# A hybrid decoder step on one core: nine matmuls that nothing reads, another order of the first loads, and sums of squares on GpSimd

## The chip, the cores and the metric

The kernel runs on one core of a Trainium2 chip. A core has five engines that run side by side, each with its own list of instructions: TensorE (PE, matmuls; PEld is its weight load), VectorE (DVE), ScalarE (ACT), GpSimd (POOL) and SyncE (SP), which here issues almost all DMA transfers. They wait for each other by semaphores. The metric is the device time of one execution in microseconds (us).

## What is computed

One inference step of a one-layer decoder on 1056 tokens: 1024 prompt tokens, and 8 sequences of 4 sampled tokens. The part that matters here is the very beginning of the layer:

```
h    = x * rsqrt(mean(x*x) + eps) * norm1        # RMSNorm over 1024 channels
proj = h @ w_in                                  # 1024 -> z | x,B,C | dt | q | k | v
```

After it come a Mamba-2 head group (a short causal convolution, then a chunked scan), a sliding-window attention group, one output projection with the residual, a second RMSNorm, an up-projection with a short convolution and a gate, and a down-projection. Everything is in float32.

## The kernel before

**Precision and layout.** Activations stand with channels on the partitions: `x[k]` is a block of 128 channels by T = 1056 tokens, k = 0 to 7. Each operand of a large matmul is split into a high and a low part: ScalarE writes the high part with a Copy (`xh` of the activations, L182; `uh` of the weights, L116), VectorE writes what is left over (`xl`, L183; `ul`, L119), and `dense` (L147) issues three matmuls for each product: high by high, low by high, high by low.

**The opening (L207 to L245).** The normalization is not applied ahead of the projection. The projection starts on the raw rows times the norm's weight, and the factor 1/rms of each token is applied to its results. So two things are made in the same loop over the eight k:

- the split rows: `xr` is loaded (L222), ScalarE makes `xh` with the norm's weight from `colt` as its scale, VectorE makes `xl`. For k = 0 this goes in three pieces of PC = 352 tokens, for the others in one of 1056;
- the sum of squares: ScalarE squares `xr` into `sq` (L228; the first one straight into `ssum`, L225), and an addition puts it onto `ssum` (L229). `sq` has two buffers, so a third square has to wait until the first has been added.

Two units of weights (`w01`, 128 output channels each) are loaded in parts of 256 columns, one part of each for every second k, and split by `load_part` (L113 to L119).

The matmuls of these two units run k by k: for each k two units by three pieces of tokens by three products, 18 matmuls of 128x352, 144 in all. They write the PSUM tiles called `ps` and `two`. Behind them `stats` (L155) sums `ssum` over the channels with nine matmuls that have one column, VectorE makes `rstd` of it, and TensorE goes on with the key and value projection (`token_major`, L199), whose weights (`wkv`, three loads) use the same two `raw` buffers as `w01` did.

**What sets the order.** The program is written in the order of the source, and a scheduler then places the instructions of each engine by its own estimate of times, before the kernel is built. So a change at the start can move instructions much later in the program. Around the middle a list called `PLAN` sets in which order the scan, the convolution, the gates and parts of the output projection are put to the scheduler. In the up-projection (L989) `half_rstd` (sums at L851, broadcast at L858) belongs to the second RMSNorm of one half of the tokens.

**The very first instructions.** VectorE fills `ones` (L207). ScalarE does one Exp of a single column (L208), ahead of which its function table is loaded. SP issues the two weight parts of k = 0, then `colt`, then the three pieces of the first rows, then the rest (L115, L218, L222).

Of the kernel before, what the change touches and what calls it, by code (L numbers as in the profile page):

```python
# [9 lines left out]
F32 = mybir.dt.float32  # L10
F32R = mybir.dt.float32r
I32 = mybir.dt.int32
AF = mybir.ActivationFunctionType
ALU = mybir.AluOpType
# [4 lines left out]
T = 1056  # L19
NP = 1024  # L20
NS = 32
NB = 8
NPAIR = 22
EPS = 1e-6
NEG = -1e30
PC = 352
# [20 lines left out]
def kernel(ctx, tc, xT, wxbc, wkv, wq, wz, wout, wup, wdn, cols, rows, cst, idm,  # L47
# [3 lines left out]
    act, dve, pool, pe, sp = nc.scalar, nc.vector, nc.gpsimd, nc.tensor, nc.sync  # L51
# [6 lines left out]
    xpc, xp = opened("xp", bufs=8, side="right")  # L58
    yp = ctx.enter_context(tc.tile_pool(name="yp", bufs=8))
# [6 lines left out]
    pqc, pq = opened("pq", bufs=3, space=PSUM)  # L66
# [4 lines left out]
    def bank(p=None):  # L71
        if p is None:
            p = pm if pm2 is None or rot[0] % 8 < 3 else pm2
            rot[0] += 1
        return p.tile([128, 512], F32, tag="ps", name="ps")
# [4 lines left out]
    colt = const.tile([128, NCOL], F32, name="colt")  # L80
# [5 lines left out]
    ones = const.tile([128, 128], F32, name="ones")  # L86
    rstd_bc = mid.tile([128, T], F32, name="rstd_bc")
    rstd = const.tile([128, 9], F32, name="rstd")
# [20 lines left out]
    def unit():  # L109
        return (wr.tile([128, 1024], F32, tag="raw", name="raw"), wp.tile([128, 1024], F32R, tag="uh", name="uh"),  # L110
                wp.tile([128, 1024], F32R, tag="ul", name="ul"))

    def load_part(u, src, a, b, e=None):  # L113
        raw, hi, lo = (t[:, a:b] for t in u)
        sp.dma_start(out=raw, in_=src)  # L115
        act.activation(out=hi, in_=raw, func=AF.Copy)  # L116
        n = (b - a) // (1 if e else 1)
        for i in range(0, b - a, n):
            (e or dve).tensor_tensor(out=lo[:, i:i + n], in0=raw[:, i:i + n], in1=hi[:, i:i + n].bitcast(F32),  # L119
                                     op=ALU.subtract)  # L120
# [52 lines left out]
    def x_pair(p):  # L173
        return (p.tile([128, T], F32R, tag="xh", name="xh"), p.tile([128, T], F32R, tag="xl", name="xl"))
# [30 lines left out]


    dve.memset(ones, 1.0)  # L207
    act.activation(out=rstd[:, 0:1], in_=ones[:, 0:1], func=AF.Exp)  # L208
    x = [None] * 8
    with tc.tile_pool(name="st", bufs=1, side="right", reuse_waits="tile") as stp:  # L210
        ssum = stp.tile([128, T], F32, name="ssum")
        w01 = [unit(), unit()]
        for k in range(8):
            if k % 2 == 0:
                for m in range(2):
                    load_part(w01[m], wxbc[m][:, 128 * k:128 * k + 256], 128 * k, 128 * k + 256)
            if k == 0:
                sp.dma_start(out=colt, in_=cols)  # L218
            xr = yp.tile([128, T], F32, tag="y", name="xr")
            x[k] = x_pair(xp)  # L220
            for a, b in ([(0, PC), (PC, 2 * PC), (2 * PC, T)] if k == 0 else [(0, T)]):
                sp.dma_start(out=xr[:, a:b], in_=xT[k][:, a:b])  # L222
                split(xr[:, a:b], x[k], col(C_N1 + k), a, b)
            if k == 0:
                act.activation(out=ssum, in_=xr, func=AF.Square)  # L225
            else:
                sq = stp.tile([128, T], F32, tag="sq", name="sq", bufs=2)
                act.activation(out=sq, in_=xr, func=AF.Square)  # L228
                dve.tensor_tensor(out=ssum, in0=ssum, in1=sq, op=ALU.add)  # L229
        w01 = [u[1:] for u in w01]  # L230
        sp.dma_start(out=idt, in_=idm)
        wkvu = [load_unit(wkv[:, 3 * i:min(8, 3 * i + 3), :].rearrange("p k c -> p (k c)"), 264 * min(3, 8 - 3 * i))
                for i in range(3)]
        sp.dma_start(out=sstt, in_=sst)
        sp.dma_start(out=rowt, in_=rows)
        sp.dma_start(out=cs, in_=cst[:, 0:K_LOW])
        dve.tensor_scalar(out=chalf, in0=colt[:, C_CW:C_CW + 40], scalar1=0.5, scalar2=None, op0=ALU.mult)
        two = pc.tile([128, 2, 512], F32, tag="sc", name="two")
        ps01 = [[bank(pm) for _ in range(3)], [two[:, 0], two[:, 1], bank(pq)]]
        for k in range(8):  # L240
            for m in range(2):
                for p in range(3):
                    dense(ps01[m][p][:, :PC], wl(w01[m]), xr_(x, p), [k], first=k == 0, last=k == 7)
                if k == 7 and m == 0:
                    stats(stp, ssum, pq)  # L245
        kv0 = token_major(264, wkvu, 3, 0, bank(pq))
        bcast(pq)
# [52 lines left out]
    with tc.tile_pool(name="at", bufs=1, reuse_waits="tile") as at:  # L300
# [52 lines left out]
        with tc.tile_pool(name="kv", bufs=1, reuse_waits="tile") as kvp:  # L353
# [4 lines left out]
            for t in range(9):  # L358
                _, m = tw(t)
# [4 lines left out]
                                         in1=rowt[:m, R_DTB:R_DTB + 8], op0=ALU.mult, op1=ALU.add)  # L364
# [12 lines left out]
                              op=ALU.add)  # L377
# [6 lines left out]
                              op=ALU.mult)  # L384
            sp.dma_start(out=pk, in_=kall[:, 7, :])
            sp.dma_start(out=sk[:, 124:128, :], in_=kall[:NS, 8, :])
            for j in range(3):
                ps = bank(pq)
                ts_ = range(4 * j, min(9, 4 * j + 4))
                for i, t in enumerate(ts_):  # L390
                    _, m = tw(t)
                    pe.transpose(out=ps[:, i * 128:i * 128 + m], in_=kall[:m, t, :], identity=ident[:m, :m])
                a = 512 * j
# [23 lines left out]
            for j in (13, 11, 9, 7, 5, 3):  # L417
# [9 lines left out]
                              in1=b3(na.unsqueeze(1), 128, 9, 8), op=ALU.mult)  # L427
# [14 lines left out]
                      start=True, stop=True)  # L442
# [391 lines left out]
    ssum = [None, None]  # L834
# [424 lines left out]
```

## Time and profile before

| what | us |
|---|---|
| time, median of three runs | 1193.34 |
| lowest and highest of them | 1191.61, 1196.62 |
| the profiled execution, its own time | 1193.78 |
| span of the profiled execution, from its first to its last instruction | 1192.0 |
| busy in it: PE, DVE, ACT, POOL | 1150.6, 872.0, 504.7, 316.6 |

The profiled execution takes 1.8 us more than its span. A row of the timeline has the start in us from the span's start, the busy time in us, the engine, the line of the source, the operation, what it writes and reads, how many such instructions were merged (x), and in brackets the idle time of the engine just before and what ended it. A row of the windows has a stretch of time, its length, the busy time and the number of instructions of PE, PEld, DVE, ACT and POOL, the clock that TensorE was granted (1.00 is full), the busy share of the DMA engines and GB/s. Matmuls are pipelined, so the rate of TensorE is read from the distance between two starts and not from the duration of one.

### The profile page before, as it was taken

Reading aid. Unit: us, or ns where it says so; the run is one execution under the profiler, and the core shown is the slowest. Engines: PE = TensorE matmul, PEld = TensorE weight load, DVE = VectorE, ACT = ScalarE, POOL = GpSimd, SP = SyncE. Lnnn points to the kernel's source line nnn. Section 1 sums busy time; section 2 is a strip of 40 time slices with the busy share of each in tenths; the row PEclk is TensorE's granted clock in tenths of the full one; section 3 lists DMA queues with packets and bytes.
Section 4 is the critical chain, followed back from the end, with each engine's and each line's share of the span. In section 5 each row is a group of like instructions: output and inputs, shape, how many; then the busy total and the mean of one; then the engine's idle time right before and its main releaser. Section 6 shows DMA issues by size and latency. Waiting matters only on the chain.

```text
span 1192.0 us, 22098 instructions
## 1 busy us (share of the span) xinstructions
PE 1150.6 (97%) x8614; PEld 1108.3 (93%) x8614; DVE 872.0 (73%) x1755; ACT 504.7 (42%) x992; POOL 316.6 (27%) x455
## 2 busy tenths in 40 slices
PE   8999999989968999889999999999999999999998
PEld 8998888879957999789999999999999999999998
DVE  7678967566987578998776666666666787677764
ACT  7444544445462334555455554545454421112110
POOL 0123233143454000044343444434442111001000
PEclk9999999999999999999999999999999999999999
DMA  8111112122454523122222222222222944324203
GB/s 294 64 63 54 36 37 59 51 90 87 142 195 154 174 81 120 36 93 74 85 82 81 73 90 73 90 73 89 73 74 89 364 144 155 105 90 128 96 9 146
DMA packets 52361, 122.53 MB, mean 103 GB/s; under 512 B 9232, under 2 KB 19984, under 8 KB 52240
## 3 DMA queue, kind: packets, MB, share of 16 engines
q1 hardware_dynamic: 52256, 121.12, 29.6%
q8 instruction: 67, 1.10, 0.4%
q14 instruction: 38, 0.31, 0.1%
HBM read 94.86 MB, written 27.26 MB: 102 GB/s over the span
## 4 chain that ended last, share of the span: by engine, by line
PE 86%; DVE 9%; ACT 2%; issue 2%; DMA 1%; POOL 0%; SPq 0%; ACTq 0%; DVEq 0%
PE ps L147 39%; PE ps L989 32%; PE ps L199 6%; PE ps L525 1%; PE sc L503 1%; DVE au L935 1%; DVE x2l L883 1%; PE two L147 1%; DVE c L1031 1%; DMA raw<-in_wup 1%; PE ps L517 1%; PE yy L653 1%; PE st L660 0%; DMA gr<-gd 0%; PE px L611 0%
## 5 line engine op out<-in xcount | busy, mean ns | idle before, releaser
L989 PE MATMUL ps<-x2h,au 128*128 128x264 f32 x2464 | 456.6, 286 | 10.2 <-ACT au L934 3.1
L989 PEld LDWEIGHTS ps<-x2h,au 128*128 128x128 f32 x2464 | 383.8, 189 | 13.1 <-ACT au L934 4.0
L989 PE MATMUL ps<-x2l,au 128*128 128x264 f32 x1232 | 348.7, 285 | 0.2 <-DVE x2l L883 0.2
L989 PEld LDWEIGHTS ps<-x2l,au 128*128 128x128 f32 x1232 | 232.4, 189 | 0.6 <-DVE x2l L883 0.6
L1104 DVE TENSOR_TENSOR acc<-acc,ps 128x352 f32<-128x352 f32 x264 | 131.4, 518 | 66.4 <-PE ps L147 65.9
L147 PE MATMUL ps<-xh,uh 128*128 128x264 f32 (+3 forms) x528 | 164.1, 317 | 8.8 <-ACT xh L182 5.8
L147 PE MATMUL ps<-gh,ul 128*128 128x352 f32 x528 | 170.1, 322 | 0.0
L147 PE MATMUL ps<-gl,uh 128*128 128x352 f32 x528 | 170.0, 322 | 0.0
L147 PE MATMUL ps<-gh,uh 128*128 128x352 f32 x528 | 167.9, 322 | 1.1 <-ACT gh L179 1.1
L147 PE MATMUL ps<-xl,uh 128*128 128x264 f32 (+3 forms) x528 | 165.6, 314 | 0.0
L147 PE MATMUL ps<-xh,ul 128*128 128x264 f32 (+3 forms) x528 | 165.1, 313 | 0.0
L116 ACT ACTIVATE uh<-raw 128x1024 fp32r<-128x1024 f32 (+3 forms) x59 | 55.8, 953 | 193.6 <-PE ps L147 169.4
L1031 DVE SCALAR_TENSOR_TENSOR c<-u,colt,c 128x1072 f32<-128x1072 f32 x88 | 121.6, 1383 | 6.5 <-ACT c L1029 6.1
L147 PEld LDWEIGHTS ps<-xh,uh 128*128 128x128 f32 x528 | 101.3, 193 | 12.6 <-ACT xh L182 5.8
L935 DVE TENSOR_TENSOR au<-raw,au 128x512 fp32r<-128x512 f32 x115 | 80.0, 711 | 40.4 <-ACT au L934 40.2
L147 PEld LDWEIGHTS ps<-xl,uh 128*128 128x128 f32 x528 | 102.1, 193 | 1.8 <-POOL xl L180 0.4
L147 PEld LDWEIGHTS ps<-xh,ul 128*128 128x128 f32 x528 | 102.1, 193 | 1.5 <-issue 0.8
L147 PEld LDWEIGHTS ps<-gh,uh 128*128 128x128 f32 x528 | 98.8, 188 | 1.3 <-ACT gh L179 1.3
L147 PEld LDWEIGHTS ps<-gl,uh 128*128 128x128 f32 x528 | 99.2, 188 | 0.4
L147 PEld LDWEIGHTS ps<-gh,ul 128*128 128x128 f32 x528 | 99.3, 188 | 0.0
L934 ACT ACTIVATE au<-raw 128x512 fp32r<-128x512 f32 x115 | 71.1, 625 | 31.0 <-POOL raw L922 11.9
L119 DVE TENSOR_TENSOR ul<-raw,uh 128x1024 fp32r<-128x1024 f32 (+3 forms) x51 | 62.3, 1231 | 10.8 <-ACT uh L116 10.8
(295 smaller groups left out, 1884.2 us busy)
## 6 DMA issues: line engine op xcount, KB each, us to landing
raw<-in_wup SPq DMA_DIRECT2D x46, 512.0 KB, 3.6
gr<-gd SPq DMA_DIRECT2D x22, 528.0 KB, 5.3
gd<-c SPq DMA_DIRECT2D x22, 512.0 KB, 2.6
raw<-in_wdn SPq DMA_DIRECT2D x22, 512.0 KB, 3.6
raw<-in_wout SPq DMA_DIRECT2D x12, 512.0 KB, 3.5
acc<-in_xT SPq DMA_DIRECT2D x16, 264.0 KB, 5.4
accd<-acc SPq DMA_DIRECT2D x16, 264.0 KB, 2.6
acc<-accd SPq DMA_DIRECT2D x8, 528.0 KB, 8.8
```

The source lines that it names most:

```text
L116: act.activation(out=hi, in_=raw, func=AF.Copy)
L119: (e or dve).tensor_tensor(out=lo[:, i:i + n], in0=raw[:, i:i + n], in1=hi[:, i:i + n].bitcast(F32), op=ALU.subtract)
L147: pe.matmul(out=ps, lhsT=w(a, k), rhs=x(b, k), start=first and k == ks[0] and i == 0, stop=last and k == ks[-1] and i == 2)
L199: pe.matmul(out=ps[:m, :n], lhsT=x[k][c][:, a:a + m], rhs=w[k // nk][b][:, o:o + n], start=k == 0 and i == 0, stop=k == 7 and i == 2)
L503: pe.matmul(out=sb[:, v, c].rearrange("p i k -> p (i k)"), lhsT=qT[a][r, c], rhs=kT[b][r, o:o + 256], start=i == 0, stop=i == 2)
L517: pe.transpose(out=pt[:, h], in_=P[:, h], identity=ident)
L525: pe.matmul(out=po[64 * v:64 * v + 64, 0:256].rearrange("p (c q) -> p c q", c=2), lhsT=(vall[:, t - i] if i or not t else vdif[:, t - 1])[ ...
L934: act.activation(out=u[:, 0:512], in_=src, func=AF.Copy)
L935: dve.tensor_tensor(out=u[:, 512:1024], in0=src, in1=u[:, 0:512].bitcast(F32), op=ALU.subtract)
L989: pe.matmul(out=ps, lhsT=wgt[:, 512 * a + 128 * k:512 * a + 128 * k + 128], rhs=xx[b][:, k], start=opens and k == 0 and i == 0, stop=k == ...
L1031: dve.scalar_tensor_tensor(out=c[:, 0:n], in0=u[:, j:j + n], scalar=col(C_FW + 3 * m + j), in1=c[:, 0:n], op0=ALU.mult, op1=ALU.add)
L1104: dve.tensor_tensor(out=o, in0=o, in1=ps[:, :PC], op=ALU.add)
```

## The change

1. Ahead of everything TensorE gets nine matmuls of `ones` by `ones`, 128x128, into a PSUM tile that nobody reads.
2. The two weight parts of k = 0 are issued from ScalarE's queue, ahead of its table load. SP issues the first third of the first rows first, then `colt`, then the other two thirds.
3. In the source, the splits of the first weights now stand ahead of the splits of the first rows and behind the load of the first third; for the even k from 2 on the order of weights and rows stays.
4. The additions of squares of k = 1 to 5 go to GpSimd; those of k = 6 and 7 stay on VectorE.

```diff
+NWARM = 9
...
     def load_part(u, src, a, b, e=None):
         raw, hi, lo = (t[:, a:b] for t in u)
-        sp.dma_start(out=raw, in_=src)
+        if src is not None:
+            sp.dma_start(out=raw, in_=src)
         act.activation(out=hi, in_=raw, func=AF.Copy)
...
     dve.memset(ones, 1.0)
-    act.activation(out=rstd[:, 0:1], in_=ones[:, 0:1], func=AF.Exp)
     x = [None] * 8
+
+    idle = bank(pq)
+    for i in range(NWARM):
+        pe.matmul(out=idle[:, 0:128], lhsT=ones, rhs=ones, start=True, stop=True)
     with tc.tile_pool(name="st", bufs=1, side="right", reuse_waits="tile") as stp:
         ssum = stp.tile([128, T], F32, name="ssum")
         w01 = [unit(), unit()]
+        for m in range(2):
+            act.dma_start(out=w01[m][0][:, 0:256], in_=wxbc[m][:, 0:256])
+        act.activation(out=rstd[:, 0:1], in_=ones[:, 0:1], func=AF.Exp)
         for k in range(8):
-            if k % 2 == 0:
+            xr = yp.tile([128, T], F32, tag="y", name="xr")
+            x[k] = x_pair(xp)
+            if k == 0:
+                sp.dma_start(out=xr[:, 0:PC], in_=xT[k][:, 0:PC])
+                sp.dma_start(out=colt, in_=cols)
+                for m in range(2):
+                    load_part(w01[m], None, 0, 256)
+            elif k % 2 == 0:
                 for m in range(2):
                     load_part(w01[m], wxbc[m][:, 128 * k:128 * k + 256], 128 * k, 128 * k + 256)
-            if k == 0:
-                sp.dma_start(out=colt, in_=cols)
-            xr = yp.tile([128, T], F32, tag="y", name="xr")
-            x[k] = x_pair(xp)
             for a, b in ([(0, PC), (PC, 2 * PC), (2 * PC, T)] if k == 0 else [(0, T)]):
-                sp.dma_start(out=xr[:, a:b], in_=xT[k][:, a:b])
+                if k or a:
+                    sp.dma_start(out=xr[:, a:b], in_=xT[k][:, a:b])
                 split(xr[:, a:b], x[k], col(C_N1 + k), a, b)
...
-                dve.tensor_tensor(out=ssum, in0=ssum, in1=sq, op=ALU.add)
+                (pool if k < 6 else dve).tensor_tensor(out=ssum, in0=ssum, in1=sq, op=ALU.add)
```

The new lines push all later lines 12 further down in the source (L147 is L149 after the change, L222 is L234, L229 is L241, L851 is L863).

SP's queue at the start of the program, before (`raw` are the weight parts, `xr` the rows, pieces of 352 or a whole block of 1056):

```order
L115 DMA raw<-in_wxbc 128x256 x2
L218 DMA colt<-in_cols 128x241
L222 DMA xr<-in_xT 128x352 x3
L222 DMA xr<-in_xT 128x1056
L115 DMA raw<-in_wxbc 128x256 x2
L222 DMA xr<-in_xT 128x1056 x2
```

and now:

```order
L225 DMA xr<-in_xT 128x352
L226 DMA colt<-in_cols 128x241
L234 DMA xr<-in_xT 128x352 x2
L234 DMA xr<-in_xT 128x1056
L117 DMA raw<-in_wxbc 128x256 x2
L234 DMA xr<-in_xT 128x1056 x2
```

The first two weight parts have left the queue, so that every transfer behind them stands two places further ahead; the rest has kept its order.

VectorE at the start of the program, before (`ul` and `xl` are the low parts of weights and rows, `ssum<-ssum,sq` the additions of squares):

```order
L119 TENSOR_TENSOR ul<-raw,uh 128x256
L237 TENSOR_SCALAR chalf<-colt 128x40
L119 TENSOR_TENSOR ul<-raw,uh 128x256
L183 SCALAR_TENSOR_TENSOR xl<-xr,colt,xh 128x352 x3
L183 SCALAR_TENSOR_TENSOR xl<-xr,colt,xh 128x1056
L229 TENSOR_TENSOR ssum<-ssum,sq 128x1056
L119 TENSOR_TENSOR ul<-raw,uh 128x256 x2
L183 SCALAR_TENSOR_TENSOR xl<-xr,colt,xh 128x1056
L229 TENSOR_TENSOR ssum<-ssum,sq 128x1056
```

and now:

```order
L249 TENSOR_SCALAR chalf<-colt 128x40
L121 TENSOR_TENSOR ul<-raw,uh 128x256
L185 SCALAR_TENSOR_TENSOR xl<-xr,colt,xh 128x352
L121 TENSOR_TENSOR ul<-raw,uh 128x256
L185 SCALAR_TENSOR_TENSOR xl<-xr,colt,xh 128x352 x2
L185 SCALAR_TENSOR_TENSOR xl<-xr,colt,xh 128x1056
L121 TENSOR_TENSOR ul<-raw,uh 128x256 x2
L185 SCALAR_TENSOR_TENSOR xl<-xr,colt,xh 128x1056 x2
```

The first rows' low part has moved between the two weight parts, and the additions between the low parts are gone; GpSimd has five of them in a row, directly ahead of its first subtraction of weights.

TensorE much later, at the sums of the second RMSNorm for the second half of the tokens (`ps<-ones,ssum` are the sums, the others are matmuls of the up-projection), before:

```order
L851 MATMUL ps<-ones,ssum_5166 88x1 x5
L989 MATMUL ps<-x2h,au 128x264
L989 MATMUL ps<-x2l,au 128x264
L989 MATMUL ps<-x2h,au 128x264 x2
L989 MATMUL ps<-x2l,au 128x264
L989 MATMUL ps<-x2h,au 128x264 x2
L989 MATMUL ps<-x2l,au 128x264
L989 MATMUL ps<-x2h,au 128x264 x2
L989 MATMUL ps<-x2l,au 128x264
L989 MATMUL ps<-x2h,au 128x264
L851 MATMUL ps<-ones,ssum_5166 88x1
```

and now:

```order
L1001 MATMUL ps<-x2l,au 128x264
L1001 MATMUL ps<-x2h,au 128x264 x2
L1001 MATMUL ps<-x2l,au 128x264
L1001 MATMUL ps<-x2h,au 128x264
L863 MATMUL ps<-ones,ssum_5176 88x1 x6
L1001 MATMUL ps<-x2h,au 128x264
L1001 MATMUL ps<-x2l,au 128x264
```

The six sums now stand together, behind more of the up-projection. From the 145th matmul of the before kernel to the middle of the scan TensorE's order is unchanged; from there to the early up-projection it differs in many small places like this one, and behind them it is the same again.

## The prediction

> **What bounds the kernel now.** I read the page first, then TensorE's waits in the opening, then the opening by windows and by timeline.
>
> ```profile
> PE 1150.6 (97%) x8614; PEld 1108.3 (93%) x8614; DVE 872.0 (73%) x1755; ACT 504.7 (42%) x992; POOL 316.6 (27%) x455
> PE 86%; DVE 9%; ACT 2%; issue 2%; DMA 1%; POOL 0%; SPq 0%; ACTq 0%; DVEq 0%
> ...
> PE ps L147 <- ACT xh L182: 5.8, 1, 5.8
> ```
>
> TensorE is busy for 97% of the span and is 86% of the chain that ended last. Of the 41.4 us in which it is idle, the first 5.8 us are the wait for the first rows. This and the rate of the first matmuls are what the change can touch directly, and all that it can save in the opening lies within these rows:
>
> ```profile
> 0.00:5.80 5.80, 0.00 (x0) 0.00 (x0) 1.17 (x8) 2.96 (x6) 0.69 (x7) 1.00 0.63 172
> 5.80:10.90 5.10, 5.10 (x19) 5.10 (x19) 2.38 (x4) 3.93 (x5) 0.00 (x0) 1.00 0.93 325
> 10.90:31.20 20.30, 20.30 (x128) 20.16 (x127) 20.11 (x23) 16.22 (x22) 0.00 (x0) 1.00 0.79 302
> 31.20:33.13 1.93, 1.93 (x21) 1.90 (x19) 0.00 (x0) 0.10 (x1) 0.00 (x0) 1.00 0.82 194
> 33.13:39.53 6.40, 5.93 (x35) 5.44 (x33) 3.45 (x18) 2.81 (x6) 2.71 (x5) 0.73 0.42 147
> ```
>
> The columns after the length are PE, PEld, DVE, ACT, POOL, the clock, the DMA share and GB/s. From 5.80 TensorE never stops until the sums at 31.20. But VectorE is busy 20.11 of 20.30 us beside it: two engines are full here, not one. TensorE's starts show the rate:
>
> ```profile
> 5.80 0.66 PE L147 MATMUL ps<-xh,uh 128*128 128x352 f32 x1 [5.80 <-ACT xh L182]
> ...
> 8.90 0.49 PE L147 MATMUL ps<-xl,uh 128*128 128x352 f32 x1
> 9.20 0.49 PE L147 MATMUL ps<-xh,ul 128*128 128x352 f32 x1
> 10.90 0.64 PE L147 MATMUL ps<-xh,uh 128*128 128x352 f32 x3
> 11.71 0.32 PE L147 MATMUL ps<-xl,uh 128*128 128x352 f32 x1
> 13.79 0.64 PE L147 MATMUL ps<-xh,uh 128*128 128x352 f32 x3
> 16.81 0.64 PE L147 MATMUL ps<-xh,uh 128*128 128x352 f32 x3
> 19.68 0.64 PE L147 MATMUL ps<-xh,uh 128*128 128x352 f32 x3
> 31.20 1.99 PE L155 MATMUL ps<-ones,ssum 128*128 128x1 f32 x18
> ```
>
> At 8.90 two starts are 0.30 us apart. The 18 matmuls of k = 0 take 5.80 to 10.90, 5.10 us; those of k = 3 take 16.81 to 19.68, 2.87 us or 0.159 each. The first 4.6 us or so run at half rate, though the clock column reads 1.00 there. Behind the sums it happens again, and there the column does show it (0.73 over 6.40 us, which costs 0.27 x 6.40 = 1.7 us).
>
> Does the slow start cost its 5.10 - 2.87 = 2.23 us? That depends on when the rows of k = 1 are there:
>
> ```profile
> 2.11 1.85 SPq L222 DMA_DIRECT2D xr<-in_xT  x4
> ...
> 0.73 1.28 ACT L208 ACT_TABLE_LOAD   x1 [0.73 <-PEq L1234]
> 2.86 0.94 ACT L116 ACTIVATE uh<-raw 128x256 fp32r<-128x256 f32 x2 [0.63 <-DMA raw<-in_wxbc]
> 5.16 1.07 ACT L182 ACTIVATE xh<-xr,colt 128x352 fp32r<-128x352 f32 x2 [1.36 <-DMA xr<-in_xT]
> 7.22 0.59 ACT L182 ACTIVATE xh<-xr,colt 128x352 fp32r<-128x352 f32 x1 [1.00 <-DMA xr<-in_xT]
> 7.72 1.07 ACT L225 ACTIVATE ssum<-xr 128x1056 f32<-128x1056 f32 x1
> 8.96 1.18 ACT L182 ACTIVATE xh<-xr,colt 128x1056 fp32r<-128x1056 f32 x1 [0.17 <-DMA xr<-in_xT]
> 10.04 1.07 ACT L228 ACTIVATE sq<-xr 128x1056 f32<-128x1056 f32 x1
> ...
> 10.17 1.32 DVE L183 SCALAR_TENSOR_TENSOR xl<-xr,colt,xh 128x1056 fp32r<-128x1056 f32 x1 [1.74 <-ACT xh L182]
> ```
>
> ScalarE waits for the last third of k = 0 until 7.22 and for the rows of k = 1 until 8.96. Their high part is ready at 10.14, their low part at 10.17 + 1.32 = 11.49. TensorE takes up that low part at 11.71, five matmuls into k = 1: it arrives just in time. So the slow matmuls of k = 0 are almost wholly hidden behind the loading of rows. The point that bounds the opening is 11.49, a DMA followed by ScalarE and VectorE.
>
> **The change part by part.**
>
> *Nine idle matmuls.* In the row at 31.20 a float32 matmul leaves two records: 18 for nine, in 1.93 us, 0.107 each, with 128 columns of weights to load. The nine new ones are 18 records too. Their price is at least 18 x 0.107 = 1.9 us, and 3.9 us if at half rate everything takes twice as long. They need only `ones`, ready at 1.0 us, so they end between 2.9 and 4.9 us, while TensorE would wait for rows anyway: cost nothing. Without that cover they would cost these 1.9 to 3.9 us. If 4.6 us of work release the full rate, as at the first matmuls, k = 0 runs fast from about 5.6 on.
>
> *Loads.* SP issues one transfer in about 0.45 us (1.85 us for four). The rows of k = 1 were its seventh transfer, issued at 2.11 + 3 x 0.46 = 3.5; now they are its fifth, at 0.74 + 4 x 0.45 = 2.55, so 0.95 us earlier, and so is the last third of k = 0. On ScalarE two issues at SP's price push the table load from 0.73 to about 1.6 and the first weight split from 2.86 to about 3.1; it has waited for its rows until 5.16, so this is covered. The weights are no later, since they are still issued at 0.74. How much earlier do the rows land? No earlier if the DMA engines are the limit: the bytes ahead of them are the same, and in 5.80:10.90 their share is 0.93. At most 0.95 us if the issue is the limit. In the first window it is 0.63 over 5.8 us, including the start, so some time is free: I take 0.6 us. Then the last third comes at 6.6, ScalarE's squares follow, the high part of k = 1 is ready at 9.5, the low part at 10.9. TensorE starts with the first rows at about 5.2 (their bytes share the engines with the weights), has finished k = 0 at about 8.8, and then waits for ScalarE and VectorE. This is the new wait: a fast TensorE meets rows that come only 0.6 us earlier. Gain 0.6 us, and not 2.23.
>
> *Additions on GpSimd.* VectorE loses five of seven additions:
>
> ```profile
> L229 DVE TENSOR_TENSOR ssum<-ssum,sq 128x1056 f32<-128x1056 f32 x7 | 8.8, 1254 | 0.1
> L119 POOL TENSOR_TENSOR ul<-raw,uh 128x1024 fp32r<-128x1024 f32 x8 | 19.1, 2391 | 37.4 <-ACT uh L116 37.2
> L922 POOL TENSOR_TENSOR t<-t,raw 128x512 f32<-128x512 f32 x20 | 28.5, 1425 | 88.6 <-DVE au L935 88.6
> ```
>
> That is 5 x 1.25 = 6.3 us, from 20.11 to 13.8 of 20.30. The only stall that this can remove is at k = 2: 13.79 to 16.81 is 3.02 us against 2.87, so 0.15 us.
> On GpSimd one addition costs 1056/1024 x 2.391 = 2.47 us by the first row, 1056/512 x 1.425 = 2.94 us by the second, whose stage has a busy VectorE as here. I take 2.94. The first square is ready at 11.1 - 0.6 = 10.5, so the fifth addition ends at 10.5 + 5 x 2.94 = 25.2. ScalarE's last square waits for it (`sq` has two buffers; behind it are the first splits of `wkv`): 26.3. VectorE's two additions end at 26.3 + 1.25 = 27.6. TensorE wants the sum at 31.20 - 0.75 = 30.4: 2.8 us to spare. The splits of rows for k = 6 and 7 stand ahead of the squares that wait. So this is hidden, cost nothing.
>
> *What follows.*
>
> ```profile
> 28.26 1.84 ACT L116 ACTIVATE uh<-raw 128x792 fp32r<-128x792 f32 x2 [2.88 <-DMA raw<-in_wkv]
> 33.03 0.64 ACT L116 ACTIVATE uh<-raw 128x528 fp32r<-128x528 f32 x1 [2.93 <-DMA raw<-in_wkv]
> ```
>
> The next weights, `wkv`, waited for a DMA, which waits until VectorE frees the `raw` buffers. VectorE gets there earlier now, so they come at least as early as TensorE does.
>
> *Order further on.* The scheduler has moved many instructions in the scan and the early up-projection. TensorE is not always busy there:
>
> ```profile
> 320.00:340.00 20.00, 15.88 (x118) 13.25 (x118) 14.74 (x24) 13.18 (x34) 10.21 (x16) 0.91 0.78 251
> 340.00:360.00 20.00, 15.14 (x145) 12.31 (x143) 19.87 (x49) 11.16 (x31) 9.78 (x13) 1.00 0.34 118
> 480.00:500.00 20.00, 16.36 (x116) 15.33 (x115) 19.30 (x34) 10.82 (x22) 0.00 (x0) 0.91 0.15 54
> 500.00:520.00 20.00, 15.79 (x121) 14.73 (x119) 18.48 (x30) 12.88 (x20) 4.82 (x6) 1.00 0.15 54
> ```
>
> It is idle 4.1 + 4.9 + 3.6 + 4.2 = 16.8 us, beside a VectorE that is nearly full in three of the four. The same work in another order can win or lose a part of this; I allow a fifth, 3.4 us, to either side, and take zero.
>
> **Sum.** Against the profiled execution: 1193.78 - 0.6 - 0.15 = 1193.03. It stands 0.44 above the median of 1193.34, so the forecast is 1192.6 us. This is far inside 0.5% (6 us, about what a measurement of this kernel can tell from no change).
>
> **The rivals.**
>
> *Rows come no earlier (chance 0.15).* Ends at 1193.34 - 0.15 = 1193.2. For it: the share of 0.93 in 5.80:10.90. Against it: the idle DMA time ahead of 5.80. [...] No run here shows yet which of the two it is. The same end comes if the idle matmuls do not release the clock: k = 0 from 5.2 at 0.29 each ends at 10.4, and little of the 0.6 is left.
>
> *The slow start counts in full (0.12).* If rows came as early as TensorE wants them, it would save 2.23 us of slow matmuls and 5.80 - 4.8 = 1.0 us of waiting: 1193.34 - 3.2 = 1190.1. For that the low part of k = 1 would have to be ready at 8.3 and its rows at 5.8, where now they land at 8.96. Against it: two transfers fewer in SP's queue do not give 3 us.
>
> *The order further on decides (0.15).* 3.4 us to either side: 1189.2 or 1196.0.
>
> *GpSimd holds up the sums (0.08), slower than before.* From 10.5 + 5 d + 1.07 + 1.25 = 30.4 on, which is d = 3.5 us an addition, TensorE waits at the sums and everything behind waits with it. Each further 0.1 us of d costs 0.5 us; at d = 4.9 it is 6.9 us, 1192.6 + 6.9 = 1199.5. For it: GpSimd shares the stretch with a VectorE at work, and its 128x512 row is slower there. Against it: even that row gives 2.94.
>
> **How the numbers follow.** The forecast case has 0.50. The range goes from the full slow start with an order that helps, 1190.1 - 3.1 = 1187.0, to no gain with an order that hurts, 1193.3 + 3.4 = 1196.7. Faster by over 0.5% means under 1187.4, which only two favourable cases together reach: 0.10. Slower by over 0.5% means over 1199.3: GpSimd, or an order that does worse than I allow: 0.07. The rest, 0.83, is the same.
>
> **What would show it.** Right: 18 records of idle matmuls that end before 5; matmul starts 0.16 apart from about 5.6; a wait of TensorE for `xh` or `xl` of k = 1 near 9 to 11; the sums near 30.4; GpSimd's additions under 3.5 us each and VectorE near 14 us in that stretch. Wrong: a TensorE that goes through k = 1 without a wait at full rate (the second rival); starts still 0.29 apart at 8 us; a wait of the sums (L157) for VectorE's additions; or an opening that is shifted by 0.75 us and an end that is not, which puts the cause into the order further on.

## The result and the profile after

The changed kernel takes 1207.4 us (median of six, 1201.2 to 1211.8), the kernel before 1191.2 (six): a ratio of 1.0122, 95% interval 1.0093 to 1.0151 (the two medians alone divide to 1.0136). A second series gave 1207.8 and 1.0131 (1.0097 to 1.0165). Single executions of some kernels fell to a clock of 0.65 to 0.85; they count in the medians of the table below, but not in its ratios, its half-rate loss or its stages, and so one of its rows has no stages. The changed kernel is slower by 1.2%; the forecast was "the same", and its range ended at 1196.7. The profiled execution takes 1206.67 us, its span is 1204.9 against 1192.0.

The opening by windows, changed kernel, cut where TensorE starts the first rows, takes up the low part of k = 1, starts the sums and leaves them:

```profile
0.00:5.33 5.33, 4.21 (x18) 3.92 (x18) 0.74 (x7) 2.54 (x5) 0.70 (x7) 1.00 0.69 203
5.33:10.64 5.31, 4.61 (x24) 3.98 (x24) 3.27 (x6) 4.79 (x8) 0.35 (x1) 1.00 0.97 351
10.64:37.67 27.03, 21.58 (x122) 21.27 (x122) 24.78 (x17) 15.77 (x21) 13.88 (x5) 0.87 0.63 233
37.67:39.59 1.92, 1.92 (x20) 1.89 (x18) 0.00 (x0) 0.46 (x1) 0.00 (x0) 1.00 0.48 166
```

Up to the low part of k = 1 the change does what it says: 10.64 against 11.71 us before. The same matmuls then take 27.03 us; before, 31.20 - 11.71 = 19.49. TensorE is idle for 5.45 of them and its clock is 0.87. VectorE should have been relieved; it is busy 24.78 us with fewer instructions than before. TensorE's waits up to the sums name it:

```profile
PE ps L149 <- DVE xl L185: 5.7, 2, 5.4
...
PE ps L149 <- ACT xh L184: 0.4, 1, 0.4
```

And the timelines of VectorE and of GpSimd, changed kernel, tell why (start, busy, engine, line, operation, what it writes and reads, how many merged):

```profile
9.27 1.32 DVE L185 SCALAR_TENSOR_TENSOR xl<-xr,colt,xh 128x1056 fp32r<-128x1056 f32 x1 [2.04 <-ACT xh L184]
10.54 5.24 DVE L121 TENSOR_TENSOR ul<-raw,uh 128x256 fp32r<-128x256 f32 x2
15.71 6.90 DVE L185 SCALAR_TENSOR_TENSOR xl<-xr,colt,xh 128x1056 fp32r<-128x1056 f32 x2
22.53 3.01 DVE L121 TENSOR_TENSOR ul<-raw,uh 128x256 fp32r<-128x256 f32 x2
25.47 2.54 DVE L185 SCALAR_TENSOR_TENSOR xl<-xr,colt,xh 128x1056 fp32r<-128x1056 f32 x2
...
10.29 5.21 POOL L241 TENSOR_TENSOR ssum<-ssum,sq 128x1056 f32<-128x1056 f32 x2 [9.06 <-ACT sq L240]
15.65 9.28 POOL L241 TENSOR_TENSOR ssum<-ssum,sq 128x1056 f32<-128x1056 f32 x3 [0.15 <-ACT sq L240]
```

Read the two engines side by side. The two small `ul` subtractions last 10.54 to 15.78, GpSimd's first two additions 10.29 to 15.50. The two `xl` of 15.71 to 22.61 stand beside the next additions. GpSimd ends at 24.93, and from 25.47 on two `xl` take 2.54 us again, 1.27 each. A short VectorE instruction that meets an addition on GpSimd lasts here until that addition is over: the two `ul` take 2.66 and 2.65 us, where two of the same size took 0.42 us each ahead of the additions (4.72 and 5.81), and each ends 0.28 us after the addition that it met.

The kernel before shows the same thing at two places, neither of which the prediction read. VectorE and GpSimd, kernel before:

```profile
63.54 3.13 DVE L119 TENSOR_TENSOR ul<-raw,uh 128x1024 fp32r<-128x1024 f32 x1 [2.26 <-ACT uh L116]
...
63.18 2.40 POOL L119 TENSOR_TENSOR ul<-raw,uh 128x1024 fp32r<-128x1024 f32 x1
...
93.59 2.30 DVE L140 SCALAR_TENSOR_TENSOR qv<-rs 128x8 f32<-128x8 f32 x1
...
93.46 2.41 POOL L119 TENSOR_TENSOR ul<-raw,uh 128x1024 fp32r<-128x1024 f32 x1 [0.82 <-ACT uh L116]
```

An instruction with eight columns that takes 2.30 us, and ends 0.02 us after GpSimd does (95.89 and 95.87), is not at work: it is waiting inside its own busy time. (The same instruction takes 0.17 us at 80.09, with no GpSimd instruction beside it.)

Behind the opening the trace is later by another 6.4 us. Windows from the sums to the scan, to the end of it and of the output projection, to the end of the up-projection, and to the end; kernel before, then the changed one:

```profile
31.20:279.00 247.80, 239.46 (x1759) 214.10 (x1757) 176.51 (x537) 116.04 (x318) 70.08 (x107) 0.97 0.18 57
279.00:463.80 184.80, 172.53 (x1410) 159.91 (x1410) 142.46 (x343) 82.98 (x180) 47.80 (x73) 0.98 0.43 140
463.80:934.50 470.70, 459.22 (x3722) 455.72 (x3721) 341.32 (x521) 240.11 (x419) 180.51 (x252) 1.00 0.24 85
934.50:1192.00 257.50, 254.00 (x1588) 253.36 (x1586) 188.06 (x322) 42.48 (x44) 17.51 (x17) 1.00 0.37 131
```

```profile
37.67:284.80 247.13, 238.19 (x1759) 212.69 (x1757) 178.21 (x537) 115.39 (x318) 70.20 (x107) 0.98 0.18 56
284.80:474.70 189.90, 178.23 (x1410) 163.25 (x1410) 141.03 (x343) 81.67 (x179) 50.13 (x73) 0.96 0.41 136
474.70:947.40 472.70, 461.09 (x3722) 457.84 (x3721) 335.45 (x521) 242.05 (x420) 184.53 (x252) 0.99 0.26 85
947.40:1204.90 257.50, 253.97 (x1588) 253.33 (x1586) 188.65 (x322) 42.48 (x44) 17.90 (x17) 1.00 0.37 131
```

The opening costs 37.67 - 31.20 = 6.5 us, the scan 5.1, the up-projection 2.0; from the sums to the scan 0.7 comes back. In the scan TensorE is not idle for longer (11.7 us against 12.3); it is busy for longer, at a lower clock (0.96 against 0.98). This is where the scheduler has put TensorE's instructions in another order.

### The profile page after: what moved, and what is told of

It reads as the page before. It is cut to its first block, busy times and chain, and to the rows that moved or that the text cites. A ratio compares the mean times of both kernels' runs of the same rounds, so it can differ in the third digit from the quotient of the medians.

```text
span 1204.9 us, 22147 instructions
## 1 busy us (share of the span) xinstructions
PE 1161.9 (96%) x8632; PEld 1116.3 (93%) x8632; DVE 872.1 (72%) x1750; ACT 504.7 (42%) x992; POOL 337.7 (28%) x460
## 4 chain that ended last, share of the span: by engine, by line
PE 85%; DVE 8%; DMA 3%; ACT 2%; issue 1%; POOL 0%; SPq 0%; DVEq 0%; ACTq 0%; POOLq 0%
PE ps L149 38%; PE ps L1001 33%; PE ps L201 6%; DMA raw<-in_wup 1%; PE ps L537 1%; PE sc L515 1%; DVE au L947 1%; DVE x2l L895 1%; PE yy L665 1%; PE st L672 1%; PE ps L529 1%; PE two L149 1%; DMA h<-in_h0T 1%; PE yy L667 0%; DVE acc L882 0%
## 5 line engine op out<-in xcount | busy, mean ns | idle before, releaser
L149 PE MATMUL ps<-xl,uh 128*128 128x264 f32 (+3 forms) x528 | 166.6, 316 | 7.6 <-DVE xl L185 5.7
L149 PE MATMUL ps<-gh,ul 128*128 128x352 f32 x528 | 170.1, 322 | 0.0
L149 PE MATMUL ps<-gl,uh 128*128 128x352 f32 x528 | 170.0, 322 | 0.0
L149 PE MATMUL ps<-xh,uh 128*128 128x264 f32 (+3 forms) x528 | 163.8, 316 | 5.6 <-ACT uh L118 1.9
L149 PE MATMUL ps<-gh,uh 128*128 128x352 f32 x528 | 167.9, 322 | 0.6 <-ACT gh L181 0.6
L149 PE MATMUL ps<-xh,ul 128*128 128x264 f32 (+3 forms) x528 | 164.9, 313 | 0.0
L149 PEld LDWEIGHTS ps<-xl,uh 128*128 128x128 f32 x528 | 102.6, 194 | 11.2 <-DVE xl L185 6.3
L149 PEld LDWEIGHTS ps<-xh,uh 128*128 128x128 f32 x528 | 101.1, 193 | 10.6 <-issue 2.8
L149 PEld LDWEIGHTS ps<-xh,ul 128*128 128x128 f32 x528 | 102.4, 194 | 1.0 <-issue 0.2
L149 PEld LDWEIGHTS ps<-gh,uh 128*128 128x128 f32 x528 | 98.8, 188 | 0.9 <-ACT gh L181 0.9
L149 PEld LDWEIGHTS ps<-gl,uh 128*128 128x128 f32 x528 | 99.2, 188 | 0.4
L149 PEld LDWEIGHTS ps<-gh,ul 128*128 128x128 f32 x528 | 99.3, 188 | 0.0
L121 DVE TENSOR_TENSOR ul<-raw,uh 128x1024 fp32r<-128x1024 f32 (+3 forms) x51 | 65.2, 1287 | 10.1 <-ACT uh L118 10.1
```

The source lines that it names most:

```text
L149: pe.matmul(out=ps, lhsT=w(a, k), rhs=x(b, k), start=first and k == ks[0] and i == 0, stop=last and k == ks[-1] and i == 2)
```

## The experiments

**Theory A**: while an addition runs on GpSimd, VectorE's two-input instructions cannot run, so an addition costs VectorE's path GpSimd's 2.9 us in place of its own 1.25. **Theory B**: the new order of loads stretches VectorE. **Theory C**: the other order further on costs the rest, whatever the opening does. All runs of the decoder stand in one table; ratios are against the kernel before on the same chip. The three columns of stages are from one profile each, and a profiled execution can lie several us from its kernel's median (1206.6 against 1201.5 with the additions alone, 1188.5 against 1192.7 with the idle matmuls alone). The half-rate loss is the mean over the runs of (1 - granted clock) x span.

| kernel | median us | ratio (95%) | sums at | sums to scan | scan to end of up-proj. | half-rate loss |
|---|---|---|---|---|---|---|
| before | 1191 to 1193 | | 31.2 | 247.8 | 655.5 | 13 |
| changed | 1207.4 | 1.0122 (1.0093-1.0151) | 37.7 | 247.1 | 662.6 | 23.3 |
| changed, again | 1207.8 | 1.0131 (1.0097-1.0165) | 37.7 | 249.7 | 659.2 | 21.9 |
| before + additions on GpSimd | 1201.5 | 1.0074 (1.0049-1.0100) | 38.5 | 249.9 | 659.0 | 17.6 |
| two additions on GpSimd | 1203.6 | 1.0100 (1.0075-1.0125) | 34.1 | 250.0 | 660.3 | 18.6 |
| additions in quarters | 1200.7 | 1.0084 (1.0054-1.0115) | 34.5 | 247.0 | 658.5 | 18.0 |
| additions of one column | 1196.2 | 1.0034 (1.0015-1.0054) | 30.3 | 247.6 | 658.8 | 16.2 |
| one-input on GpSimd | 1197.5 | 1.0052 (1.0031-1.0073) | 30.1 | 246.7 | 661.7 | 17.3 |
| additions back on VectorE | 1188.5 | 0.9972 (0.9953-0.9990) | | | | 13.4 |
| the same, again | 1188.0 | 0.9965 (0.9949-0.9980) | 30.7 | 246.4 | 650.7 | 12.4 |
| loads only | 1191.1 | 0.9985 (0.9969-1.0002) | 30.8 | 244.7 | 653.8 | 13.9 |
| the same + k = 1 in thirds | 1190.2 | 0.9982 (0.9969-0.9994) | 30.3 | 247.7 | 655.0 | 13.4 |
| idle matmuls only | 1192.7 | 1.0000 (0.9977-1.0022) | 31.3 | 245.0 | 653.0 | 14.3 |

Behind the opening TensorE has one order of instructions in the changed kernel and in the kernels with additions in quarters, of one column and with one input, and another in the kernel before, with the idle matmuls alone and with k = 1 in thirds. The kernels with the additions alone, with two additions, and with the additions back on VectorE (with and without idle matmuls) have three further orders there.

### Additions back on VectorE, and the additions alone

```diff
-                (pool if k < 6 else dve).tensor_tensor(out=ssum, in0=ssum, in1=sq, op=ALU.add)
+                dve.tensor_tensor(out=ssum, in0=ssum, in1=sq, op=ALU.add)
```

> The changed kernel with all seven additions of squares back on VectorE; idle matmuls and new load order stay. Theory A (GpSimd's additions keep VectorE's two-input instructions out while they run: 0.38 us became 2.6, 1.3 became 3.45): VectorE's subtractions take 0.38 and 1.3 us again, TensorE's 5.4 us wait for the low part of k = 2 is gone, sums at 30 to 30.7 us instead of 37.67 (before: 31.20). Theory B (the new order of loads, not GpSimd, stretches VectorE: more transfers in flight beside it): VectorE stays stretched, sums near 37. Theory C (the scheduler's other order further on costs the other 6.4 us whatever the opening does): sums as in A, but the whole is still 4 to 7 us above the kernel before; by A alone it is 0 to 2 us below it, 1189 to 1191.

Repeated:

> The changed kernel with all additions on VectorE once more, for a profile at the usual clock. Theory A: VectorE's subtractions at 0.38 and 1.3 us, sums at 30.0 to 30.7; total 2 to 5 us below the kernel before as the first time.

The sums stand at 30.70, and VectorE, with the new loads beside it and 1.25 us more to do for each k, is quick again (timeline of the repeat):

```profile
10.89 1.25 DVE L241 TENSOR_TENSOR ssum<-ssum,sq 128x1056 f32<-128x1056 f32 x1
12.05 0.75 DVE L121 TENSOR_TENSOR ul<-raw,uh 128x256 fp32r<-128x256 f32 x2
12.73 1.31 DVE L185 SCALAR_TENSOR_TENSOR xl<-xr,colt,xh 128x1056 fp32r<-128x1056 f32 x1
```

The reverse edit puts only the additions of k = 1 to 5 of the kernel before on GpSimd:

```diff
-                dve.tensor_tensor(out=ssum, in0=ssum, in1=sq, op=ALU.add)
+                (pool if k < 6 else dve).tensor_tensor(out=ssum, in0=ssum, in1=sq, op=ALU.add)
```

> The kernel before with only the additions of k = 1 to 5 on GpSimd. Theory A: each addition keeps VectorE out for 2.9 us instead of using it for 1.25, 5 x 1.65 = 8.2 us on a VectorE that was busy 20.11 of 20.30 us: sums at 37.5 to 39.5 us, total 6 to 15 us slower than before. Theory B (loads): VectorE at 0.38 and 1.3 us, sums at 31.2, total the same within 2 us.

With the old loads VectorE is held as in the changed kernel, and the sums stand at 38.5 (timelines of VectorE and GpSimd):

```profile
11.52 5.22 DVE L119 TENSOR_TENSOR ul<-raw,uh 128x256 fp32r<-128x256 f32 x2
16.67 6.93 DVE L183 SCALAR_TENSOR_TENSOR xl<-xr,colt,xh 128x1056 fp32r<-128x1056 f32 x2
...
11.26 5.21 POOL L229 TENSOR_TENSOR ssum<-ssum,sq 128x1056 f32<-128x1056 f32 x2 [10.03 <-ACT sq L228]
16.64 9.31 POOL L229 TENSOR_TENSOR ssum<-ssum,sq 128x1056 f32<-128x1056 f32 x3 [0.17 <-ACT sq L228]
```

The additions alone make the loss of the opening, and the loads have no part in it. Theory B has fallen. What lies behind the sums cannot be compared so directly here, since this kernel has an order of its own there.

### Two additions, and additions in quarters

```diff
-                (pool if k < 6 else dve).tensor_tensor(out=ssum, in0=ssum, in1=sq, op=ALU.add)
+                (pool if k < 3 else dve).tensor_tensor(out=ssum, in0=ssum, in1=sq, op=ALU.add)
```

> The changed kernel with only the additions of k = 1 and 2 on GpSimd. Theory A, additive: 2 x 1.65 = 3.3 us on VectorE, sums at 33 to 34 us, between 30.3 (none) and 37.67 (five). Rival D (the loss is one event: the first long wait takes TensorE's clock, and the rest follows from that): sums near 37 already with two, or near 31 if two are not enough to make TensorE wait.

Sums at 34.13. From 30.70 with none, two additions cost 3.4 us, 1.7 each; the sum by A was 2 x 1.65 = 3.3. TensorE waits 3.3 us for the low part of k = 2 here and keeps its clock up to the sums, so the wait alone, without a loss of clock, shifts the opening: rival D has fallen. Its total (+11 us) is not explained by that; it has yet another order further on, and the longest way from the sums to the scan in the table (250.0).

```diff
-                (pool if k < 6 else dve).tensor_tensor(out=ssum, in0=ssum, in1=sq, op=ALU.add)
+                for c in range(0, T if k < 6 else 0, 264):
+                    pool.tensor_tensor(out=ssum[:, c:c + 264], in0=ssum[:, c:c + 264], in1=sq[:, c:c + 264], op=ALU.add)
+                if k > 5:
+                    dve.tensor_tensor(out=ssum, in0=ssum, in1=sq, op=ALU.add)
```

> The changed kernel with each addition on GpSimd cut into four pieces of 264 columns; the order of all other instructions is the changed kernel's. Theory A (exclusive use, one instruction at a time): no VectorE instruction is held longer than a quarter addition, 0.75 us and its own time, but GpSimd's total is the same or a little more, so the sums stay at 36.5 to 39 us. Rival E (VectorE is slowed only because it starves behind one long instruction, and shares well with short ones): sums at 31 to 33 us and most of the loss gone.

The sums come at 34.48, between the two expectations. GpSimd's and VectorE's timelines and TensorE's waits:

```profile
10.00 21.68 POOL L242 TENSOR_TENSOR ssum<-ssum,sq 128x264 f32<-128x264 f32 x20 [8.78 <-ACT sq L240]
...
12.01 3.54 DVE L185 SCALAR_TENSOR_TENSOR xl<-xr,colt,xh 128x1056 fp32r<-128x1056 f32 x2
15.47 1.88 DVE L121 TENSOR_TENSOR ul<-raw,uh 128x256 fp32r<-128x256 f32 x2
...
PE ps L157 <- DVE ssum L244: 2.8, 1, 2.8
PE ps L149 <- DVE xl L185: 1.4, 3, 0.7
```

Now the two engines take turns: `xl` takes 1.77 us instead of 3.45, and GpSimd is the one that is held, 21.68 us for what takes 14.5 in whole additions. TensorE waits only 1.4 us for low parts on its way through the rows, and stops for 2.8 us at the sums instead. Cutting the instructions moved the wait here, it did not remove it: both engines' work still lies end to end.

### What holds what

A kernel of its own, which computes nothing of the decoder, puts four VectorE instructions of one kind beside three GpSimd instructions of one kind.

> Nothing of the decoder is computed: four VectorE instructions of one kind stand beside three GpSimd instructions of one kind, 128x1056 float32, for six kinds of VectorE and four of GpSimd, and each kind alone. Theory A: subtraction and scaled subtraction on VectorE take 1.25 to 1.35 us alone and, beside GpSimd's addition, last as long as GpSimd's (2.5 to 3.5 us); beside GpSimd's one-input kinds and its fill they stay at 1.25 to 1.35. Multiplication with a PSUM input, one-input kinds and the fill on VectorE keep their time beside any of GpSimd's. Theory B (VectorE was stretched by transfers, not by GpSimd): no pair differs from VectorE alone by more than a tenth.

Its rows, VectorE first alone and then beside GpSimd's addition (128x1056; 128x512 where PSUM is read):

```profile
6.16 5.14 DVE L69 TENSOR_TENSOR vo<-va,vb 128x1056 f32<-128x1056 f32 x4
18.27 2.94 DVE L76 TENSOR_SCALAR vo<-va 128x1056 f32<-128x1056 f32 x4
25.76 2.87 DVE L82 TENSOR_TENSOR vo<-pt,va 128x512 f32<-128x512 f32 x4
...
43.37 11.40 DVE L69 TENSOR_TENSOR vo<-va,vb 128x1056 f32<-128x1056 f32 x4
67.82 9.20 DVE L76 TENSOR_SCALAR vo<-va 128x1056 f32<-128x1056 f32 x4
87.82 2.87 DVE L82 TENSOR_TENSOR vo<-pt,va 128x512 f32<-128x512 f32 x4
...
108.69 7.36 DVE L69 TENSOR_TENSOR vo<-va,vb 128x1056 f32<-128x1056 f32 x4
193.30 5.14 DVE L69 TENSOR_TENSOR vo<-va,vb 128x1056 f32<-128x1056 f32 x4
205.72 5.14 DVE L76 TENSOR_SCALAR vo<-va 128x1056 f32<-128x1056 f32 x4
```

and GpSimd's addition, alone and beside VectorE's subtraction:

```profile
35.25 7.38 POOL L88 TENSOR_TENSOR po<-pa,pb 128x1056 f32<-128x1056 f32 x3
...
43.53 10.12 POOL L88 TENSOR_TENSOR po<-pa,pb 128x1056 f32<-128x1056 f32 x3
```

Alone VectorE needs 5.14 us and GpSimd 7.38; together they need 11.40, not 7.38. Two-input subtraction is held (5.14 to 11.40), and so, against the expectation, is an instruction with one input (2.94 to 9.20). A multiplication that reads PSUM is not (2.87 both times). The row at 108.69 stands beside GpSimd's multiplication with one input, which holds VectorE as well (7.36 us against 5.14), for its shorter time (three of them take 3.38 us alone). Beside GpSimd's fill, which reads nothing, the subtraction is free (193.30: 5.14 us, as alone), the one-input instruction is not (205.72: 5.14 us against 2.94). So theory A is right in its core and too narrow in its kinds. What the held pairs share in the hardware is not shown by these rows.

### GpSimd at work, but harmless

Two kernels keep the order of the changed kernel, but for four swaps of TensorE's in the opening, and take the long additions away. Both thereby leave most of the squares out of the sum, and the normalization that follows from it is not the decoder's.

```diff
-                (pool if k < 6 else dve).tensor_tensor(out=ssum, in0=ssum, in1=sq, op=ALU.add)
+                if k < 6:
+                    pool.tensor_tensor(out=ssum[:, 0:1], in0=ssum[:, 0:1], in1=sq[:, 0:1], op=ALU.add)
+                else:
+                    dve.tensor_tensor(out=ssum, in0=ssum, in1=sq, op=ALU.add)
```

> The changed kernel with the five additions on GpSimd cut to one column of 1056 (the sums of squares of k = 1 to 5 are left out except for the first token). TensorE's and VectorE's order of instructions stays that of the changed kernel but for four swaps inside the opening, so only the long GpSimd instructions are gone. Theory A: VectorE at 0.38 and 1.3 us, sums at 29.8 to 30.7 us, 7 us before the changed kernel's. Theory C (the order further on costs what is left, whatever the opening does): sums as in A, but from the sums to the end 6 us more than in the kernel before, so a total of 1196 to 1198 us. Theory C2 (the later loss hangs on how the clock's half-rate stretches fall, and the delayed opening sets that): from the sums to the end as in the kernel before, total 1189 to 1192.

The sums stand at 30.28, 7.4 us before the changed kernel's, and the total is still 1196.2, which is what C expected; C2 has fallen. From the sums to the end the medians give 1196.2 - 1.8 - 30.3 = 1164.1 us, against 1192.0 - 1.8 - 31.2 = 1159.0 before: 5.1 more. Its rows of the scan and the up-projection:

```profile
277.90:464.80 186.90, 177.34 (x1410) 162.09 (x1410) 139.32 (x343) 81.92 (x179) 48.90 (x73) 0.96 0.42 139
464.80:936.70 471.90, 459.82 (x3723) 456.12 (x3722) 336.40 (x521) 241.43 (x420) 183.42 (x252) 0.99 0.25 85
```

The other kernel puts an instruction of full width with one input there:

```diff
-                (pool if k < 6 else dve).tensor_tensor(out=ssum, in0=ssum, in1=sq, op=ALU.add)
+                if k < 6:
+                    pool.tensor_scalar(out=ssum, in0=sq, scalar1=1.0, scalar2=1.0, op0=ALU.mult, op1=ALU.mult)
+                else:
+                    dve.tensor_tensor(out=ssum, in0=ssum, in1=sq, op=ALU.add)
```

> The changed kernel with the five additions on GpSimd replaced by a multiplication of the square by one, written to the same tile (a single tensor as input, full width; the squares of k = 0 to 4 are left out of the sum). Order as in the changed kernel but for four swaps in the opening. Theory A in its narrow form (only a GpSimd instruction with two tensor inputs keeps VectorE out): VectorE at 0.38 and 1.3 us, sums at 29.8 to 30.7. Theory A in its wide form (any long GpSimd instruction on SBUF does it): VectorE held for the length of GpSimd's instructions again, sums by 1.65 us or less per instruction later, 33 to 37.7.

Sums at 30.12, the narrow form's number, but not by its mechanism: two `ul` take 1.58 us instead of 0.75, so VectorE is held, as the pairs show. GpSimd's instructions last 1.08 to 1.39 us, about what VectorE's addition had taken (1.25), so nothing is lost or won. This kernel does not tell the two forms apart; the pairs do.

### The other parts, and the changed kernel again

```diff
+    idle = bank(pq)
+    for i in range(9):
+        pe.matmul(out=idle[:, 0:128], lhsT=ones, rhs=ones, start=True, stop=True)
```

That is the whole edit to the kernel before.

> The kernel before with only the nine idle matmuls; every other instruction stands in the order of the kernel before. By the prediction's working a faster k = 0 meets rows of k = 1 that come no earlier (low part ready at 11.49 us): TensorE's wait moves from the rate into a wait for k = 1, sums at 31.0 to 31.2, total within 1 us of the kernel before. Rival F (the slow start counts in full): sums near 29, total 2.2 us less.

A ratio of 1.0000 and the sums at 31.3: k = 0 is done earlier and TensorE waits for k = 1. Rival F, the second rival of the prediction, has fallen. Next, the kernel with the additions back on VectorE and without the idle matmuls:

> Additions on VectorE and no idle matmuls: only the order of the loads is changed; all instructions stand in the order of the kernel with the additions back. With rows of k = 1 landing at 8.05 us their low part is ready at 10.6, and a slow k = 0 from 5.1 to 10.2 us is still done by then. Theory I (the idle matmuls buy nothing, the loads all): the same as with them within 1 us, sums 30.2 to 30.7. Rival J (both are needed): sums at 31 or later, as before, total 1191 to 1193.

Sums at 30.78 with the slow start, 30.70 without: in the opening the idle matmuls buy nothing. The total is 3.1 us higher than with them, in the same order of instructions, and inside what rival J expected (1191 to 1193); the two intervals overlap (0.9969 to 1.0002 and 0.9949 to 0.9980). It differs behind the opening, where they can do nothing that these rows show. That stays open.

```diff
-                split(xr[:, a:b], x[k], col(C_N1 + k), a, b)
+                for c in ((0, PC, 2 * PC) if k == 1 else (a,)):
+                    d = c + PC if k == 1 else b
+                    split(xr[:, c:d], x[k], col(C_N1 + k), c, d)
```

> The changed kernel with all additions on VectorE, and ScalarE and VectorE split the rows of k = 1 in three pieces of 352 as they do for k = 0 (one load). TensorE's order behind the first 45 matmuls is that of the kernel before. The first third's high part is ready 0.6 us after the rows land (8.05), the low part 0.6 later: TensorE goes on at 8.7 instead of waiting for 9.2 and 10.6. Expected: sums at 29.2 to 30.0, and with the later order of the kernel before a total of 1189 to 1191. Rival K (VectorE, not the rows of k = 1, is what TensorE waits for from there on): sums at 30.3, as without the thirds.

The sums come at 30.32, not by 30.0, which is rival K's number: the wait for k = 1 is gone, and TensorE waits 0.28 us for the high part and 0.44 for the low part of k = 2. The total is as expected. The kernel with the additions back on VectorE (0.9965) stays the fastest of all; it beats both kernels. Only 0.5 us of the 4.8 in its second series lie in the opening; the rest comes with its own order behind the sums, so it is not a gain of the loads alone.

> The changed kernel once more. From its sums (37.67 us) to the end it took 9.7 us longer than the kernel before, by the medians; three kernels with its later order but another opening took 5.1, 5.1 and 6.6 us longer there. Theory G (the later order alone sets it; the rest was scatter): 5 to 7 us behind the sums, a total of 1203 to 1206 with the kernel before at 1192. Theory H (the delayed and colder opening costs more behind the sums too): 8 to 10 us there again, 1206 to 1209.

1207.8, and 1207.8 - 1.8 - 37.7 = 1168.3 from the sums on, against 1192.8 - 1.8 - 31.2 = 1159.8: 8.5 more. That is theory H. The order does not explain everything behind the sums; the kernels with whole additions on GpSimd also take longer from the sums to the scan (247.1 to 250.0, mean 249.2; the others 244.7 to 247.8, mean 246.6; the ranges touch). A part of this is the same holding at a second place, in VectorE's chain for 1/rms behind the sums (VectorE and GpSimd, changed kernel):

```profile
41.28 2.38 DVE L142 SCALAR_TENSOR_TENSOR rs<-rs 128x9 f32<-128x9 f32 x1
...
41.26 2.38 POOL L121 TENSOR_TENSOR ul<-raw,uh 128x1024 fp32r<-128x1024 f32 x1 [16.33 <-ACT uh L118]
```

At 44.10 the same instruction takes 0.17 us. `rstd` is ready 7.2 us behind the start of the sums instead of 5.0, and TensorE, which spreads it, waits 0.7 us for it; in the other three profiles with whole additions a VectorE instruction is held in the same chain, and TensorE waits 1.9 to 2.1 us. In all other kernels GpSimd's subtraction falls outside this chain, and TensorE does not wait for `rstd`.

## Why the prediction was wrong, step by step

*Idle matmuls.* Right in what they cost and do: 18 records, 4.21 us, ended at 5.26 (bound 4.9), full rate from 6.3 (forecast 5.6), no cost and no gain in the opening.

*Loads.* Right in kind, a little small: xh of k = 1 from 8.05 instead of 8.96, low part taken up at 10.64 instead of 11.71, and the new waits of TensorE for `xh` and `xl` of k = 1 (0.4 and 0.3 us) that were foretold. With the additions on VectorE 0.4 to 0.5 us of it is left at the sums; the forecast was 0.6. The first rival, that rows come no earlier, has fallen: the rows of k = 1 came 0.91 us earlier, nearly all of the 0.95 that the issue could give, though the DMA share was 0.97 from 5.33 to 10.64.

*Additions on GpSimd: the step that failed.* "So this is hidden, cost nothing" took the two engines for independent: 6.3 us off VectorE, and GpSimd's 2.94 us hidden beside it. GpSimd's price was right (2.6 to 3.1 us each). What was wrong is that VectorE did not run beside it: a `ul` took 2.66 us instead of 0.42, an `xl` 3.45 instead of 1.3. Five additions cost VectorE GpSimd's time instead of its own, the low part of k = 2 is ready at 19.2, TensorE waits 5.45 us, loses its clock and runs at half rate (granted clock 0.50) from 19.24 to 23.2: 5.45 + 2.0 + 0.1 = 7.5 us, less the 1.07 won ahead of it, is the 6.5. The clock need not be what decides here: in the second profile of the changed kernel the half rate ended at 22.1, TensorE waited once more for a low part, until 26.88, and the sums came at the same 37.7. That points to VectorE's path. The rival on GpSimd had the wrong place too: TensorE was to wait at the sums from 3.5 us an addition on. That happened only with additions in quarters, where GpSimd takes 21.68 / 5 = 4.3 us for each. The prediction quoted a row of subtractions on GpSimd for their price and did not look at what VectorE did at those times; the rows at 63.54 and 93.59 had the answer.

*What follows.* "They come at least as early": no, VectorE frees the buffers later (the first `wkv` low part starts at 33.66 instead of 29.24). Nothing waited for it, since the sums were later still.

*Order further on.* The place was right, the size was not: 3.4 us to either side, taken as zero. From the scan to the end of the up-projection five profiles in the changed kernel's order take 658.5 to 662.6 us (mean 660.2), three in the order of the kernel before 653.0 to 655.5 (mean 654.5): 5.7 us, and no overlap. That the order does it, and not the opening, is shown by the kernel with one column. That it does so by the clock is read from the profiles, not tested: TensorE's idle time in the scan is no longer than before (11.7 and, with one column, 9.6 us against 12.3), its half-rate stretches are more. By the clock records the five profiles have 6 to 8 half-rate windows in these stages (mean 6.6), the three 3 to 5 (mean 3.7); at 1.7 us each (last section) that is 5.0 of the 5.7 us.

*The sum.* 6.5 (opening) + 5.7 (order) + about 2.6 (sums to scan, means above) = 14.8; measured 15 to 16. Of the 2.6, the waits for `rstd` are 1.7 on average; the rest stays open, and so does which of the moved instructions costs the 5.7. In the prediction's own working one bound does not add up: the lower end of the range takes 3.1 us off where the term for the order is 3.4, which would give 1186.7. It has no part in the miss.

## What to carry to other kernels

Work moved to an idle GpSimd was not moved off VectorE in these runs, where both had two SBUF inputs: nearly the sum of the two times counted (11.40 us in the pairs, of 5.14 and 7.38 alone), and GpSimd's was the longer (2.46 us an addition, against 1.29 a subtraction). Before moving, look in the trace for a VectorE instruction beside a GpSimd one and compare its time with the same instruction alone; a tiny instruction that lasts 2 us is the sign (2.30 against 0.17 in the kernel before). And an edit at the start of a scheduled program is also an edit of everything the scheduler places behind it: compare the stages one by one before crediting the whole difference to the edit.

## What was not expected of the hardware

In both profiles TensorE's granted clock changed on a grid. Worked out from windows of 1 us, the half-rate stretches of the changed kernel start at 16.38, 40.28, 272.38, 347.48, 367.96, 405.50, 501.08 and 548.86 us, all whole multiples of 3.413 us apart, and last one or two such windows; the same holds in the kernel before (34.36, 106.04, 266.47, 334.73, 385.93 and 488.33). The clock granted in them is 0.50, so each window costs half its length, 1.7 us. The changed kernel has 13 of them, the kernel before 7: 6 x 1.7 = 10.2 of the 12.9 us between the two spans. Windows with little work were followed by slow ones (changed kernel, PE's busy time first, granted clock third from the end):

```profile
12.97:16.38 3.41, 0.82 (x6) 0.53 (x4) 3.41 (x3) 3.41 (x5) 3.21 (x2) 1.00 1.03 407
16.38:19.79 3.41, 0.55 (x2) 0.55 (x3) 3.41 (x2) 3.41 (x6) 3.33 (x2) 0.50 1.18 442
340.65:344.06 3.41, 2.48 (x18) 1.21 (x16) 2.03 (x6) 2.90 (x8) 1.53 (x4) 1.00 1.03 405
344.06:347.48 3.42, 1.61 (x17) 1.00 (x16) 3.42 (x8) 1.23 (x3) 2.68 (x4) 1.00 0.61 232
347.48:350.90 3.42, 2.24 (x14) 1.22 (x10) 3.39 (x8) 0.41 (x1) 1.63 (x2) 0.50 0.39 146
364.54:367.96 3.42, 2.36 (x20) 1.78 (x16) 3.42 (x10) 2.61 (x8) 2.93 (x6) 1.00 0.15 41
388.43:391.84 3.41, 1.91 (x16) 1.67 (x15) 2.37 (x10) 0.90 (x2) 0.00 (x0) 1.00 0.41 160
```

1.8 us of idle time in one window (344.06, longest single wait 1.30) was enough; 0.9 in the window ahead of it was not. In this profile a slow window follows every window in which TensorE was busy for under 1.8 us (eight, from 12.97 to 545.45, busy for 0.39 to 1.76 us). Above that, busy time does not decide: a slow one follows 364.54, idle for 1.1 us, and none follows 388.43, idle for 1.5. One also follows the window at 36.86, which is busy throughout by the records, 1.9 us of it with the one-column sums. What exactly is counted stays open. That the same waits, cut otherwise by the grid, can cost nothing would fit the spread of several us between runs of one kernel (1201.2 to 1211.8 for the changed one); it was not tested.
